# Forward sweeps traced half a step earlier, two products ahead of the retention scores, and a bfloat16 column sum in the up projection

## The chip, the cores and the metric

One core of a Trainium2 chip runs the kernel. The metric is the device time of one execution in microseconds (us). The engines are named as in the profile: PE (TensorE matmul) and PEld (its weight loads), DVE (VectorE), ACT (ScalarE), POOL (GpSimd), SP (SyncE, which issues most transfers).

## What is computed

One block of a diffusion transformer, 2048 tokens of width 1024, with 256 context tokens. The mixer has four HGRN2 heads and four retention heads of width 128, and each head runs in both directions over the sequence. In outline:

```python
hx = rmsnorm(x, norm1_g) * (1 + sc1) + sh1            # modulated by c
feats = split(hx @ w_in)                              # q, v, gates of 4 HGRN2 and 4 retention heads
states = context_states(features of ctx)              # start states of both directions
o_f = chunk_scan(q, k, v, decay, s_f)                 # forward over the chunks
o_b = flip(chunk_scan(flip(q), flip(k), ...))         # backward
hg = rmsnorm((o_f + o_b) * sigmoid(gate)); ret = rmsnorm(y_f + y_b) * silu(gate)
x = x + g1 * (concat(hg, ret) @ w_out)
h2 = rmsnorm(x, norm2_g) * (1 + sc2) + sh2
x = x + g2 * ((silu(conv3(h2 @ w_gate)) * (h2 @ w_up)) @ w_down)
return rmsnorm(x, final_g)
```

## The kernel before

**Arithmetic.** A large product is made of pairs of float16 parts, three matmuls to a product (lines 88 to 90), and a 2x2 blocked product is done with seven block products (`unit`, `head_unit`, `ffn_unit`: products 0 to 6). Each weight is scaled by a power of two that is found from the sum of its squares: ACT squares it and accumulates a column of sums (one for each half of the weight), PE adds the column over the partitions (`allsum`, line 111, one float32 matmul with a matrix of ones for each column), and five short DVE operations make the power of two (`pow2`, lines 99 to 103).

**The heads.** A head's sequence is cut into four groups of 512 tokens. `heads` runs 32 steps, s = 4h + i: head h (0 to 3 HGRN2, 4 to 7 retention), step i of it. Step (h, i) is called h.i here. A step has three strands:

- the backward sweep of head h over group 3 - i (`hg_sweep1`, `ret_sweep1`; a generator that yields about 14 times for HGRN2 and 8 times for retention). The retention one begins with the scores (`rsc`, line 1207), the HGRN2 one with seven levels of products with K and Q (lines 837, 844, 848, 853). It leaves the output so far in a tile `ou`, the query in `qf`.
- the forward sweep of the head before, h - 1, over group i. Its first half (`hg_sweep2`, `ret_sweep2`) takes the forward state through the group (four DVE operations of line 907, eight instructions of line 905 on PE), adds the result to `ou` (line 932 or 1241), gates it (933, HGRN2), and sends it through four squares on ACT (917) and six POOL operations for the norm (`rstd`, lines 71 to 76). Its second half (`hg_sweep2b`, `ret_sweep2b`) multiplies by the norm on DVE (line 939, or four of line 1248), transposes on PE (`otp`, line 924), copies on ACT and issues a transfer on ACT's queue.
- the projection of the next step's features (`hg_proj`, `ret_proj`, or `ret_gate` near the end), the filler: a generator of some 14 or 18 products.

`step` makes the first two strands one generator, `weave` lets it run and calls the filler in between, in the proportion n_fill to n_main. `tick` puts in pieces of the next head's weights.

```python
        if prev is not None:
            (self.hg_sweep2 if hgp else self.ret_sweep2)(pool, (h - 1) % NH, i, prev)
        for j in range(3):
            next(main, None)
            yield
        ...
        if prev is not None:
            (self.hg_sweep2b if hgp else self.ret_sweep2b)(pool, (h - 1) % NH, i, prev)
        yield from main
```

What Python traces first has priority, but the order in each engine's queue is made when the program is built, by a scheduler that lets a later operation whose inputs it holds ready pass an earlier one that it holds not ready. Once built, each queue has a fixed order. Tiles of one tag share a few buffers, which come free with the last use: `tu` (three banks of PSUM, used by both sweeps, transposes and sums), `ou` and `qf` (one for each of four slots), `gate` (five).

After the 32 steps four more (head index 8) do the forward sweep of the last head alone. Then come the output projection, the up projection and the down projection.

**The up projection.** `up_weights` prepares the weights of 11 pairs of column blocks, twice each (gate and up), so it is called 22 times: two squares on ACT (line 1483), 16 matmuls of one bfloat16 column on PE (line 1488, `col`), `allsum` of the two columns of sums, the power of two, and the splitting into seven blocks. It runs as background work between the products of `ffn_unit`.

Of the kernel before, what the change touches and what calls it, by code (L numbers as in the profile page):

```python
# [11 lines left out]
BF16 = mybir.dt.bfloat16  # L12
# [3 lines left out]
ALU = mybir.AluOpType  # L16
PSUM = bass.MemoryType.PSUM

P = 128
# [4 lines left out]
NG = SEQ // G  # L24
CT = 256
NH = 4
# [24 lines left out]
def view(t, off, dims):  # L51
    return bass.AP(t.tensor, t.offset + off, [t.ap[0]] + dims)


class Kern:
# [50 lines left out]
    def allsum(self, cols, tag="tu"):  # L106

        o = self.ps(tag, [P, 1], "allsum")
        n = cols.shape[-1]
        for i in range(n):  # L110
            self.nc.tensor.matmul(o, self.onesq, cols[:, i:i + 1], start=i == 0, stop=i == n - 1, skip_group_check=True)
        return o

    def allmax(self, col, tag="tu"):
# [827 lines left out]
        nc.scalar.copy(m, tp.rearrange("p c t -> p (c t)"))  # L942
        nc.scalar.dma_start(self.mixd[h][:, g * G:(g + 1) * G], m)

    def weave(self, main, filler, n_main, n_fill):

        done = 0
        for j, _ in enumerate(main):
            while filler is not None and done * n_main < (j + 1) * n_fill:
                done += 1  # L950
                if next(filler, self) is self:
                    filler = None
        for _ in filler or ():
            pass

    def step(self, h, i, W, cur, prev, pr):

        pool = self.mp
        g = NG - 1 - i
        slot = i if h % 2 == 0 else NG - 1 - i  # L960
        hg, hgp = h < NH, h - 1 < NH
        if h < 2 * NH:
            main = (self.hg_sweep1 if hg else self.ret_sweep1)(pool, h % NH, g, slot, pr, cur)
        else:
            main = iter(())
        if prev is not None:
            (self.hg_sweep2 if hgp else self.ret_sweep2)(pool, (h - 1) % NH, i, prev)
        for j in range(3):
            next(main, None)
            yield  # L970
            if i == 0 and j == (1 if hg else 0) and h < 2 * NH:
                yield from (self.hg_context if hg else self.ret_context)(pool, h % NH, W, cur)
        if h or i:
            self.tick(self.n_tick)
        if prev is not None:
            (self.hg_sweep2b if hgp else self.ret_sweep2b)(pool, (h - 1) % NH, i, prev)
        yield from main
        if h or i:
            self.tick(self.n_tick)

    def heads(self):

        nc, pool = self.nc, self.mp
        W, items = self.W0, self.items0
        self.mod_first()
        items[5][0]()
        place = [self.gate_tile() for _ in range(4)]
        xc = self.load_rows(None, place)
        self.norm_rows(NG - 1, self.x3)
        for _, comp in items[:4]:  # L990
            comp()
        self.lower_bounds()
        self.mod1 = self.modulation(self.ep, pool, view(self.sv, V_N1, [[0, 2], [1, 8]]), self.modT[:, :, 8:16],
                                    self.modT[:, :, 0:8], 0, 1.3)
        ftags = "Kl", "Kl", "qf0", "qf1", "K0", "Q0"
        for _ in self.first_blocks(NG - 1, self.x3, self.places(ftags, "ftmp"), "pj", 1):
            pass
        for _, comp in items[4:]:
            comp()
        for w, dq in W.values():  # L1000
            nc.vector.tensor_tensor(dq, dq, self.dqx[:, 0:1], ALU.mult)
        prev, items = None, []
        cur = dict(grp={}, sg={})
        pr = {}
        first = self.hg_proj(pool, 0, NG - 1, W, pr, cur, True)
        zq = ("z",) * 7 + ("q",)
        rows = lambda g, tags: self.norm_rows(g, self.load_rows(g, [p() for p in self.places(tags, f"x{g}")]))
        x2 = rows(2, zq)
        for _ in self.with_blocks(first, self.first_blocks(2, x2, self.places(ftags, "ftmp"), "tu")):
            pass  # L1010
        Wn = W
        for s in range(4 * 2 * NH):
            h, i = divmod(s, NG)
            hn, inn = divmod(s + 1, NG)
            if i == 0:
                if h < 2 * NH - 1:
                    Wn, items = self.head_weights(h + 1)
                    n = -(-len(items) // 6)
                    if NH <= h < 2 * NH - 1:
                        mods = [it for c in ((4, 5, 6), (7, 8, 9), (10, 11))[h - NH] for it in self.mod_later(c)]  # L1020

                        pairs = [items[k:k + 2] for k in range(0, len(items), 2)]
                        none = [(None, lambda: None)] * 2
                        items = []
                        while pairs or mods:
                            items += (pairs.pop(0) if pairs else none) + (mods[:2] or none)
                            mods = mods[2:]
                        n = 4
                    self.todo += items
                else:  # L1030
                    items = self.out_weights()
                    self.todo += items[:5]
                    n = 1
                self.n_tick = n
            if i == NG - 1:
                while self.todo or self.loaded:
                    self.tick(4)
                if h == 2 * NH - 1:
                    self.todo += items[5:]
            blocks = None  # L1040
            if s == 0:
                for _ in self.first_blocks(None, self.norm_rows(None, xc), self.places(("A", "A", "Ta", "Kl"), "cftmp", 2), "tu"):
                    pass
                blocks = self.first_blocks(1, rows(1, ("ou1", "ou2", "ou3", "q", "qf2")), self.places(zq, "ftmp"), "pj")
            if s == 1:
                blocks = self.first_blocks(0, rows(0, ("ou2", "ou3", "qf2", "gate", "gate", "q")), self.places(zq, "ftmp"), "pj")
            if s == 4 * 2:
                self.ret_consts()
            prn = {}
            nxt = cur if inn else dict(grp={}, sg={})  # L1050
            if hn < 2 * NH:
                filler = (self.hg_proj if hn < NH else self.ret_proj)(pool, hn % NH, NG - 1 - inn, Wn if inn == 0 else W, prn, nxt, *((True,) if blocks else ()))
                if blocks:
                    filler = self.with_blocks(filler, blocks)
            else:
                filler = chain(self.ret_gate(NH - 1, 0, W, cur), self.ret_gate(NH - 1, 1, W, cur))
            self.weave(self.step(h, i, W, cur, prev, pr), filler, (14 if h < NH else 8) + (0 if i else 19 if h < NH else 10),
                       18 if hn < NH else 14 if hn < 2 * NH - 1 else 11 if hn < 2 * NH else 8)
            pr = prn
            if i == NG - 1:  # L1060
                prev, W, cur = cur, Wn, nxt
        for i in range(NG):
            self.weave(self.step(2 * NH, i, None, None, prev, None), self.ret_gate(NH - 1, i + 2, W, prev) if i < 2 else None, 3, 4)
            if i == 1:
                self.mixed_pairs(0)
# [403 lines left out]
    def up_weights(self, j, ty):  # L1469
# [10 lines left out]
        ssq = kp.tile([P, 2], F32, tag="ssqw2", bufs=2, name="ssqw")  # L1480
# [5 lines left out]
        for i in range(2):  # L1486
            for k in range(KT):
                nc.tensor.matmul(col[:, i:i + 1], sqs[i][:, k * P:(k + 1) * P], self.onesb, start=k == 0 and i == 0,
                                 stop=k == KT - 1 and i == 1, skip_group_check=True)
        s, neg, dq = self.scales(self.allsum(ssq, "sc"), self.dqx[:, 1:2], ("dqz", "dqvg")[ty])  # L1490

        if ty == 0:
            tap = kp.tile([P, 2, 3], F32, tag="taps", bufs=2, name="taps")
# [353 lines left out]
```

## Time and profile before

| | |
|---|---|
| median of 3 runs | 2703.32 us (2699.55 to 2703.40) |
| the profiled execution | 2701.94 us, its span 2699.5 us |
| PE busy | 94% of the span |
| heads with a forward sweep, steps 1.0 to 7.3 | 296.9 to 1238.9 us |
| last forward sweep, output projection | 1238.9 to 1521 us |
| up projection (its steady part) | 1521 to 2235 us |
| down projection | 2235 to 2699.5 us |

The boundaries are the first score matmul of a step for the heads, and rounded starts of a stage for the others. Starts and waits below are in us from the span's start. A wait is idle time of an engine just before an instruction, with the instruction that ended it behind the arrow.

### The profile page before, as it was taken

What the parts mean: (1) busy time and instruction counts of PE and PEld (TensorE: products, weight loads), DVE (VectorE), ACT (ScalarE), POOL (GpSimd) and SP (SyncE); (2) the same over time, 40 slices, a digit from 0 to 9 for tenths busy, and PEclk for the clock granted to TensorE, in tenths of its full rate; (3) what the DMA queues carried; (4) which work ended last, traced back from release to release, by engine and by line L of the source; (5) the groups of instructions that cost most, each with busy time, mean ns of one, the idle gap of its engine ahead of it and who ended that gap; (6) DMA issues with size and microseconds to landing.
All of it is one profiled execution on the core that took longest, in us unless ns stands there. A gap on an engine that the chain in (4) does not pass through costs nothing.

```text
span 2699.5 us, 56351 instructions
## 1 busy us (share of the span) xinstructions
PE 2544.2 (94%) x22829; PEld 1680.0 (62%) x22829; DVE 1847.7 (68%) x3585; ACT 1344.8 (50%) x2902; POOL 785.0 (29%) x905
## 2 busy tenths in 40 slices
PE   5798999999999999998999999999999999999998
PEld 2578888888889889886454444444444444444443
DVE  4898677776767686666466788888787777323553
ACT  5776456564555444445455566565555555311120
POOL 3733112111223232221344344343443342000102
PEclk7899999999999999998999999999999999999999
DMA  8224234243337575755521232333322325635552
GB/s 297 104 87 158 96 111 146 88 138 119 121 127 257 197 246 178 239 195 180 196 98 47 94 110 101 107 105 110 117 101 103 118 88 197 254 129 187 203 194 95
DMA packets 213621, 393.98 MB, mean 146 GB/s; under 512 B 15599, under 2 KB 97747, under 8 KB 208752
## 3 DMA queue, kind: packets, MB, share of 16 engines
q1 hardware_dynamic: 203808, 373.42, 40.1%
q10 hardware_dynamic: 9248, 16.79, 1.9%
q8 instruction: 178, 2.92, 0.4%
q14 instruction: 83, 0.68, 0.1%
q0 software_dynamic: 304, 0.17, 0.0%
HBM read 298.57 MB, written 91.75 MB: 145 GB/s over the span
## 4 chain that ended last, share of the span: by engine, by line
PE 71%; DVE 15%; ACT 4%; issue 4%; DMA 3%; POOL 2%; SPq 0%; DVEq 0%; ACTq 0%; POOLq 0%
PE pa L88 8%; PE pa L89 8%; PE pa L90 8%; PE pd L89 5%; PE pd L90 5%; PE pd L88 5%; PE pc L88 4%; PE pc L89 4%; PE pc L90 4%; PE pb L88 2%; PE pb L90 2%; PE pb L89 2%; PE opp L89 2%; PE opp L88 2%; PE opp L90 2%
## 5 line engine op out<-in xcount | busy, mean ns | idle before, releaser
L88 PE MATMUL pa<-feat,w 128*128 128x512 f16 x704 | 267.9, 381 | 12.2 <-ACT ta L549 8.1
L89 PE MATMUL pa<-feat,w 128*128 128x512 f16 x704 | 268.1, 381 | 0.0
L90 PE MATMUL pa<-feat,w 128*128 128x512 f16 x704 | 264.9, 381 | 0.0
L89 PE MATMUL pd<-wd,actl 128*128 128x512 f16 x616 | 233.3, 379 | 0.0
L90 PE MATMUL pd<-wd,actl 128*128 128x512 f16 x616 | 233.3, 379 | 0.0
L88 PE MATMUL pd<-wd,actl 128*128 128x512 f16 x616 | 232.7, 379 | 0.0
L89 PEld LDWEIGHTS <-w 128*128 128x128 f16 x1232 | 120.8, 98 | 155.4 <-issue 15.6
L90 PEld LDWEIGHTS <-w 128*128 128x128 f16 x1232 | 121.4, 99 | 145.1 <-issue 1.4
L88 PEld LDWEIGHTS <-w 128*128 128x128 f16 x1232 | 121.7, 99 | 141.6 <-issue 2.4
L89 PEld LDWEIGHTS <-hx 128*128 128x128 f16 x1824 | 183.0, 100 | 8.5 <-issue 6.3
L90 PEld LDWEIGHTS <-hx 128*128 128x128 f16 x1824 | 182.6, 100 | 3.4 <-issue 2.6
L88 PEld LDWEIGHTS <-hx 128*128 128x128 f16 x1824 | 182.9, 100 | 2.2
L1598 DVE SCALAR_TENSOR_TENSOR st<-act,modT,st 128x512 f16<-128x512 f32 x154 | 144.3, 966 | 32.3 <-ACT st L1597 32.3
L1597 ACT ACTIVATE st<-act,modT 128x512 f16<-128x512 f32 x154 | 107.2, 718 | 83.9 <-DVE act L1587 30.2
L88 PE MATMUL pa<-w_vg,hx 128*128 128x128 f16 x800 | 144.7, 222 | 0.2
L89 PE MATMUL pa<-w_vg,hx 128*128 128x128 f16 x800 | 144.5, 222 | 0.0
L90 PE MATMUL pa<-w_vg,hx 128*128 128x128 f16 x800 | 144.4, 222 | 0.0
L88 PE MATMUL pc<-feat,w 128*128 128x512 f16 x352 | 133.5, 379 | 1.3 <-ACT feat L1372 1.2
L88 PE MATMUL pa<-hx,w_z 128*128 128x256 f16 x464 | 127.6, 275 | 7.5 <-DVE rV L591 4.1
L90 PE MATMUL pc<-feat,w 128*128 128x512 f16 x352 | 133.6, 380 | 0.0
L89 PE MATMUL pc<-feat,w 128*128 128x512 f16 x352 | 133.6, 380 | 0.0
L89 PE MATMUL pa<-hx,w_z 128*128 128x256 f16 x464 | 127.3, 274 | 0.0
(551 smaller groups left out, 7557.6 us busy)
## 6 DMA issues: line engine op xcount, KB each, us to landing
hx<-hxd SPq DMA_DIRECT2D x212, 512.0 KB, 4.7
actd<-st SPq DMA_DIRECT2D x154, 256.0 KB, 2.0
actl<-actd SPq DMA_DIRECT2D x28, 1024.0 KB, 5.0
wur<-in_w_up_dram SPq DMA_DIRECT2D x44, 512.0 KB, 3.9
raw<-in_w_in_dram SPq DMA_DIRECT2D x36, 512.0 KB, 4.6
wm<-in_w_mod_dram SPq DMA_DIRECT2D x64, 256.0 KB, 4.1
hxd<-hx SPq DMA_DIRECT2D x28, 512.0 KB, 3.4
wdb<-in_w_down_dram SPq DMA_DIRECT2D x44, 256.0 KB, 3.9
```

What stands on the lines that cost most here:

```text
L88: mm(ps, lhs(0), rhs(0), start=start, stop=False, skip_group_check=True)
L89: mm(ps, lhs(0), rhs(1), start=False, stop=False, skip_group_check=True)
L90: mm(ps, lhs(1), rhs(0), start=False, stop=stop, skip_group_check=True)
L1597: nc.scalar.activation(p[:, 0], v, AF.Copy, scale=s)
L1598: nc.vector.scalar_tensor_tensor(p[:, 1], v, s, p[:, 0], ALU.mult, ALU.subtract)
```

## The change

- `step`: for heads 1 to 7 the forward sweep of group i + 1 of the head before is traced in step i, not in step i + 1: its first half after the third yield of the backward sweep, its second half at the step's end. Group 0 stays in step 0, where groups 0 and 1 are then both swept, and step 3 has no forward sweep. The four last steps (head index 8) stay as they are.
- `weave`: from head 4 on, two products of the filler are traced before the step's first operation (`lead`), and count as done.
- `up_weights`: the two columns of sums are added on DVE into one bfloat16 column (`both`), and one bfloat16 matmul with ones takes the place of the two float32 ones.

```diff
+    def allsum16(self, cols, tag):
+        both = self.wp.tile([P, 1], BF16, tag="both", bufs=2, name="both")
+        self.nc.vector.tensor_tensor(both, cols[:, 0:1], cols[:, 1:2], ALU.add)
+        o = self.ps(tag, [P, 1], "allsum")
+        self.nc.tensor.matmul(o, view(self.onesb, 0, [[0, P]]), both, start=True, stop=True, skip_group_check=True)
+        return o
...
-    def weave(self, main, filler, n_main, n_fill):
+    def weave(self, main, filler, n_main, n_fill, lead=0):
-        done = 0
+        done = lead
+        for _ in range(lead):
+            next(filler)
...
+        last = h == 2 * NH
+        sweep2, sweep2b = (self.hg_sweep2, self.hg_sweep2b) if hgp else (self.ret_sweep2, self.ret_sweep2b)
+        other = lambda sweep, k: sweep(pool, (h - 1) % NH, k, prev)
-        if prev is not None:
-            (self.hg_sweep2 if hgp else self.ret_sweep2)(pool, (h - 1) % NH, i, prev)
+        if prev is not None and (last or i == 0):
+            other(sweep2, i)
...
-        if prev is not None:
-            (self.hg_sweep2b if hgp else self.ret_sweep2b)(pool, (h - 1) % NH, i, prev)
+        if prev is not None and (last or i == 0):
+            other(sweep2b, i)
+        ahead = prev is not None and not last and i + 1 < NG
+        if ahead:
+            other(sweep2, i + 1)
         yield from main
         if h or i:
             self.tick(self.n_tick)
+        if ahead:
+            other(sweep2b, i + 1)
...
-                       18 if hn < NH else 14 if hn < 2 * NH - 1 else 11 if hn < 2 * NH else 8)
+                       18 if hn < NH else 14 if hn < 2 * NH - 1 else 11 if hn < 2 * NH else 8, 2 if h >= NH else 0)
...
-        s, neg, dq = self.scales(self.allsum(ssq, "sc"), self.dqx[:, 1:2], ("dqz", "dqvg")[ty])
+        s, neg, dq = self.scales(self.allsum16(ssq, "sc"), self.dqx[:, 1:2], ("dqz", "dqvg")[ty])
```

## Rows read from the trace of the kernel before

**Rows 1.** The page: the span, and the busy time of each engine.

```profile
span 2699.5 us, 56351 instructions
PE 2544.2 (94%) x22829; PEld 1680.0 (62%) x22829; DVE 1847.7 (68%) x3585; ACT 1344.8 (50%) x2902; POOL 785.0 (29%) x905
```

**Rows 2.** Windows: length, busy (count) of PE, PEld, DVE, ACT, POOL, clock, DMA.

```profile
296.90:792.00 495.10, 466.08 (x7665) 419.41 (x7665) 347.73 (x795) 274.94 (x688) 89.91 (x108) 0.98 0.37 121
792.00:1238.90 446.90, 422.67 (x5072) 402.23 (x5071) 309.69 (x621) 209.00 (x522) 120.22 (x131) 0.98 0.64 213
1521.00:2235.00 714.00, 709.93 (x3599) 330.57 (x3598) 574.99 (x995) 413.86 (x722) 288.92 (x192) 1.00 0.32 108
```

**Rows 3.** Waits of PE, HGRN and retention stretch: total us, times, longest.

```profile
PE sc L837 <- DVE Q L853: 10.2, 3, 3.4
PE otp L924 <- DVE ou L939: 3.2, 3, 1.9
...
PE otp L924 <- DVE ou L1248: 2.3, 1, 2.3
PE otp L924 <- DVE p2t L99: 1.6, 1, 1.6
PE rsc L1207 <- ACT rV L589: 0.7, 1, 0.7
```

**Rows 4.** Line 111 from 1400 us on: ns min/median/max, first, last start.

```profile
L111 PE MATMUL allsum<-ssqw,ones x88: 250/250/373, 1403.7 to 2228.9; 128*128 128x1 f32 x88
```

**Rows 5.** Timeline of PE at one up-projection call: start us, us, what, count.

```profile
1657.56 0.47 PE L1488 MATMUL col<-onesb,w 128*128 128x1 bf16 x13
1657.89 0.58 PE L111 MATMUL allsum<-ssqw,ones 128*128 128x1 f32 x4
1658.34 0.38 PE L90 MATMUL pb<-feat,w 128*128 128x512 f16 x1
```

**Rows 6.** Timeline of ACT and DVE at that call and the one before.

```profile
1632.08 2.06 DVE L1598 SCALAR_TENSOR_TENSOR st<-act,modT,st 128x512 f16<-128x512 f32 x3
...
1656.25 0.19 ACT L1483 ACTIVATION_READ_ACCUMULATOR w<-wur 128x1 f32 x1
1657.65 0.75 DVE L1567 SCALAR_TENSOR_TENSOR act<-ta,taps,act 128x511 f32<-128x511 f32 x1 [1.94 <-ACT act L1562]
```

**Rows 7.** Lines 907, 932, 1241 on DVE: ns min/median/max, first, last start.

```profile
L907 DVE SCALAR_TENSOR_TENSOR ou<-ou,T x32: 338/346/352, 301.7 to 825.2; 128x128 f32<-128x128 f32 x32
...
L932 DVE TENSOR_TENSOR ou<-ou,o x16: 672/679/689, 307.6 to 895.9; 128x512 f32<-128x512 f32 x16
...
L1241 DVE SCALAR_TENSOR_TENSOR ou<-o,qd,ou x16: 736/742/752, 912.1 to 1275.5; 128x512 f32<-128x512 f32 x16
```

**Rows 8.** Waits of DVE, 792 to 1238.9: total us, times, longest.

```profile
DVE ou L1248 <- POOL rs_y L76: 12.9, 10, 2.6
```

**Rows 9.** Windows by step: 2.0, 3.0, 3.1, 3.3 (HGRN), 5.0, 5.1 (retention).

```profile
463.30:519.30 56.00, 51.08 (x801) 46.21 (x800) 37.68 (x110) 36.43 (x96) 3.81 (x7) 1.00 0.23 73
626.50:680.20 53.70, 53.70 (x816) 48.60 (x815) 31.79 (x90) 23.17 (x62) 3.29 (x7) 1.00 0.23 78
680.20:719.10 38.90, 35.37 (x585) 32.02 (x584) 30.61 (x64) 20.59 (x52) 11.71 (x11) 0.96 0.39 130
...
755.00:792.00 37.00, 34.42 (x610) 31.20 (x609) 23.00 (x43) 18.57 (x47) 4.35 (x7) 1.00 0.41 141
...
908.90:941.10 32.20, 32.20 (x415) 31.13 (x414) 16.46 (x37) 12.69 (x34) 5.32 (x7) 1.00 0.46 150
941.10:971.80 30.70, 27.97 (x334) 26.11 (x333) 27.91 (x49) 14.77 (x35) 11.77 (x11) 1.00 0.73 252
```

**Rows 10.** Timeline of PE at the start of retention step 5.1.

```profile
938.59 0.27 PE L88 MATMUL pa<-hx,w_z 128*128 128x256 f16 x1
...
940.99 0.27 PE L89 MATMUL pb<-hx,w_z 128*128 128x256 f16 x1
941.10 1.06 PE L1207 MATMUL rsc<-K 128*128 128x128 f32 x8
```

More of the change, by code (lines that the diff above doesn't have):

```diff
@@ L961, in step @@
         hg, hgp = h < NH, h - 1 < NH
-        if h < 2 * NH:
+        last = h == 2 * NH
+        sweep2, sweep2b = (self.hg_sweep2, self.hg_sweep2b) if hgp else (self.ret_sweep2, self.ret_sweep2b)
+        other = lambda sweep, k: sweep(pool, (h - 1) % NH, k, prev)
+        if not last:
             main = (self.hg_sweep1 if hg else self.ret_sweep1)(pool, h % NH, g, slot, pr, cur)
@@ L970, in step @@
             yield
-            if i == 0 and j == (1 if hg else 0) and h < 2 * NH:
+            if i == 0 and j == (1 if hg else 0) and not last:
                 yield from (self.hg_context if hg else self.ret_context)(pool, h % NH, W, cur)
```

## The prediction, made before the result was known

> **What bounds the kernel now.** I read the page first, then the stages by windows, then PE's waits by stage, and only then single stretches of the timeline. PE is busy 94% of the span, the next engine, DVE, 68% [rows 1]. A change can therefore shorten the kernel in two ways: by taking PE work away, or by removing time in which PE stands still. The windows show how much there is of the second [rows 2]. In the up projection PE is busy 709.93 of 714.00 us at granted clock 1.00, so a stage with no gaps to close; only less work helps there. In the heads with forward sweeps it is busy 466.08 of 495.10 us (HGRN2) and 422.67 of 446.90 us (retention): 29.0 + 24.2 = 53.2 us idle. That is the whole stock from which moving the sweeps can take. The waits say which of it hangs on a forward sweep [rows 3]: the transpose `otp` of the second half waited for DVE for 3.2 us in the HGRN2 stretch and for 2.3 + 1.6 us in the retention one, 7.1 us together. The larger row of the HGRN2 stretch, 10.2 us for the level products behind line 853, is not the sweep's own wait; it is DVE being late with the levels.
>
> **The column sum, step by step.** The page has 88 float32 matmuls of `allsum` in this part, so four for each of the 22 calls [rows 4]: two columns, two instructions each. What they cost is read from starts, not from their 250 ns, because matmuls overlap. At one call the group of four starts at 1657.89 and the next product's matmul at 1658.34: 0.45 us of PE's queue [rows 5]. Just before, 13 `col` matmuls (bfloat16, one column, 128x128 weights, the same shape as the new one) take from 1657.56 to 1657.89, 0.33 us, 0.025 us each. The new sum is one such matmul. It saves 0.45 - 0.025 = 0.42 us a call, 22 x 0.42 = 9.2 us, and since PE has no gaps there, all of it is span. [...]
>
> The new DVE operation, one column wide, is of the size of the small ones of the power of two. DVE is busy 574.99 of 714.00 us in this stage [rows 2], so its own time is covered by 139 us of DVE idle. What counts is that the sum now waits for DVE, where before it waited for ACT alone. In half of the calls (gate side) the second square's sum is read at 1656.25 + 0.19 = 1656.44, PE comes to the sum at 1657.89, and DVE stands idle for 1.94 us up to 1657.65 [rows 6]: the addition fits in, if it stands there in DVE's queue. In the other half DVE is in a run of 0.7 us operations (three in 2.06 us) when PE arrives [rows 6]; the addition's inputs are ready long before, so it can stand earlier, but the queue's order decides. Bounds for this wait: nothing, or one such operation for 11 calls, 11 x 0.7 = 7.7 us; nothing excludes more. I take 1 us in all, near the lower end, since the sum was traced behind 16 `col` matmuls which PE reaches late.
>
> **The sweeps.** Nothing is added: the same operations stand elsewhere. A sweep costs DVE four state operations of 0.346 us and an addition of 0.679 or 0.742 us [rows 7], and then either two more 512-wide ones (HGRN2, about 0.68 each by line 932) or four more of 128 columns (retention, about 0.346 each): 3.4 to 3.5 us. For heads 1 to 7, step 0 gets a second sweep and step 3 loses its own; steps 1 and 2 keep one. Step 0 can take it: in 3.0 PE is busy all of 53.70 us with DVE at 31.79 (59%), in 5.0 all of 32.20 us with DVE at 16.46 (51%); 2.0, where PE has 4.9 us idle, is the exception [rows 9]. Step 3 is where PE idles (3.3: 37.00 - 34.42 = 2.6 us) with DVE far from full. So the two-sweep step is covered by PE's own products.
>
> The second gain is the distance between halves. DVE waits for POOL's norm before the second half: 12.9 us over ten waits in the retention stretch [rows 8], and everything behind it in DVE's queue waits too. The halves were three yields apart and are now the rest of a step apart (five yields of eight for retention, eleven of fourteen for HGRN2), so the norm should mostly be there. With it go the `otp` waits of 7.1 us. A slot's `ou` and `qf`, and the gates, also come free half a step earlier; I price that at nothing, since no row shows PE waiting for them. What is late next? PE's other just-in-time operands, above all the levels behind line 853. I let half come back: -3.6 us. Bounds: nothing, and all 7.1 us plus half of the 10.2 us (the steps that lose first-half sweep work), 12 us. The transfers of the second half are the same four per head on ACT's queue, earlier; PE waits for none of them until the output projection.
>
> **The two products ahead.** Traced earlier does not mean queued earlier. At step 5.1 the first filler product already starts at 938.59, the second runs to 940.99 and the scores start at 941.10 [rows 10]; the scheduler has done it. There is little left to gain: the wait of the scores for the value tile, 0.7 us, is the row for it [rows 3]. With the count started at two, the later calls of the filler fall on the same yields. The filler's loads, seven on SP and two on ACT's queue, move with its first call, by as little. I take nothing; bounds -0.7 and, if the scores come 24 matmuls later than now, 24 x 0.11 = 2.6 us (the spacing in rows 10, 938.59 to 941.10 for 23) in each of 15 steps, of which PE loses nothing as long as it has those matmuls to do.
>
> **The sum.** 2701.94 (the profiled execution) - 9.2 + 1.0 - 3.6 = 2690.1 us. The median of the runs stands 1.4 us above that execution, so against it the forecast is 2691.5; I say 2691.
>
> **Rivals.**
> *Only the sum counts.* The scheduler had put the sweeps where they could go, as it did with the scores, and order changes alone. Then 2701.94 - 9.2 + 1.0 = 2693.7. It lies within the forecast's own range, so I count it there.
> *The sum waits for DVE.* PE takes its matmuls in order: it idled before `otp` with products standing behind it. If `both` comes late by 0.84 us in the 11 up-side calls (a little more than one of the 0.7 us operations), 9.2 us are gone; with no gain from the sweeps the time is about 2702. [...] For it: DVE at 81% in that stage. Against: inputs ready early.
> *The sweep pushes the levels back.* The first half now stands before level 4 of HGRN2, or before the backward states of retention, in steps where DVE is nearly full: 79% in 3.1, 91% in 5.1 [rows 9]. If its 3.4 us delay what PE waits for, the 14 steps 1 and 2 of heads 1 to 7 pay. From 9.2 / 14 = 0.66 us a step the kernel is no faster; from (9.2 + 5.4) / 14 = 1.04 us it is slower than can be missed; at half the sweep's work, 1.7 us, the time is 2701.94 - 9.2 + 24 = 2717. Against it: these steps carried one sweep before too, at their beginning, and lose that one.
> *The heads give more.* The `otp` waits go whole and DVE, freed from the norm's waits, is in time for half of the level waits: 2701.94 - 9.2 - 12.2 = 2680.5.
>
> **How the numbers follow.** A difference of 0.2%, 5.4 us, is about what a measurement of this kernel can tell from no change. Forecast (2684 to 2698): 0.52. More from the heads (2676 to 2684): 0.18. Gain cancelled (2698 to 2708), by the sum's wait or by small losses in the levels: 0.18. Slower: 0.12. The range 2679 to 2703 leaves out the slower case and the outer parts of its neighbours, about 0.2. Faster is the forecast and the larger gain with a little taken off for a queue order that is new everywhere behind the first change: 0.69; same 0.19; slower 0.12.
>
> **What would show it.** In the profile after: 22 matmuls of the new line, each some 0.03 us apart from its neighbours, and no PE wait on `both`; the up projection shorter by 8 to 9 us; no `otp` waits on line 939 or 1248 in steps 1 to 3 of heads 1 to 7; DVE's waits for the norm smaller by half; PE idle in the heads at 45 to 50 us, against 53.2. The prediction is wrong if PE idles before the new sum for more than 0.4 us a call, if the level waits grow by more than the `otp` waits shrink, or if a half-clock stretch comes in or goes with the new order.

## The result and the profile after

The changed kernel took 2706.90 us (median of 20 runs, 2698.91 to 2713.83) beside 2701.53 us of the kernel before on the same chip (20 runs): ratio 1.0022, 95% interval 1.0013 to 1.0032. The forecast was 2691 us, 0.4% faster; it is 0.2% slower. The profiled execution, 2701.38 us, lies 5.5 us below that median, so its stretches show the losses rather too small.

The page of the changed kernel, span and PE's busy time (before: [rows 1]):

```profile
span 2699.6 us, 56237 instructions
...
PE 2535.8 (94%) x22763; PEld 1670.8 (62%) x22763; DVE 1851.3 (69%) x3607; ACT 1341.1 (50%) x2902; POOL 789.5 (29%) x905
```

Windows of the same three stretches (HGRN2 heads, retention heads, up projection; columns as in [rows 2]):

```profile
297.30:789.80 492.50, 464.30 (x7665) 417.00 (x7665) 343.17 (x795) 273.92 (x688) 90.40 (x108) 0.99 0.37 122
789.80:1244.40 454.60, 425.12 (x5058) 404.48 (x5057) 308.03 (x610) 208.18 (x520) 119.58 (x131) 0.97 0.63 209
1529.50:2235.10 705.60, 700.42 (x3521) 321.27 (x3520) 579.71 (x1014) 411.35 (x722) 291.15 (x192) 1.00 0.32 109
```

Against [rows 2] the HGRN2 heads gave 2.6 us and the up projection 8.4 us, close to what was forecast. The retention heads lost 7.7 us, and the lone last sweep behind them went from 22.9 (1238.9 to 1261.8) to 26.3 us (1244.4 to 1270.7). That is the whole account: 11.0 us gained, 11.1 us lost in this execution.

The clock column belongs to that account. In the retention heads nearly the same matmuls kept PE busy 2.4 us longer (425.12 for 422.67) at a granted clock of 0.97 for 0.98; the other 5.3 of the 7.7 us are idle time (29.5 for 24.2). In the HGRN2 heads PE was busy 1.8 us less, at 0.99 for 0.98, and its idle time hardly moved (28.2 for 29.0): most of that gain is shorter busy time and not closed gaps. In both traces the granted clock stands at 1.00 or at 0.50. Added up from them, 0.50 held for 17 us of the HGRN2 heads before and 7 us after, and for 14 us of the retention heads before and 24 us after. The four stretches at 0.50 in the HGRN2 heads before lie at waits of PE of 2.8 to 3.4 us, the two after at waits of 2.0 and 2.8 us. One place in the HGRN2 heads, before and after (PE's timeline, then a window; the clock is the third number from the end):

```profile
541.15 0.65 PE L837 MATMUL sc<-Q,Kl 128*32 128x32 f32 x32 [3.27 <-DVE Q L853]
541.00:544.30 3.30, 3.15 (x57) 3.09 (x58) 3.30 (x8) 0.85 (x1) 0.55 (x3) 0.50 0.24 70
```
```profile
539.53 0.46 PE L845 MATMUL sc<-Q,Kl 128*32 128x32 f32 x32 [1.98 <-DVE Q L861]
536.00:545.00 9.00, 6.54 (x135) 6.14 (x133) 9.00 (x12) 4.85 (x15) 7.63 (x8) 1.00 0.65 208
```

The waits of PE in the HGRN2 stretch (first line) and the retention stretch (the other two), against [rows 3]:

```profile
PE sc L845 <- DVE Q L861: 9.0, 7, 2.0
...
PE rob L1246 <- DVE Kt L1248: 12.2, 8, 3.0
PE pa L88 <- DVE rV L599: 11.0, 3, 4.8
```

The last two before, which [rows 3] doesn't show:

```profile
PE pa L88 <- DVE rV L591: 4.1, 2, 2.1
PE rob L1227 <- DVE Kt L1229: 3.0, 5, 1.2
```

The level waits `sc` of the HGRN2 heads add up to nearly what they did (9.0 for 10.2 us), but the longest is 2.0 us in place of 3.4. No `otp` wait is left in the retention stretch, as forecast. In their place PE waits 12.2 us for the small updates `Kt` of the backward state (3.0 before) and 11.0 us for the eviction of the value tile `rV` (4.1 before). Both are DVE's work; so the question is what DVE waited for:

```profile
DVE Q L1194 <- DMA sin<-in_rope_dram: 16.4, 6, 3.6
...
DVE ou L1267 <- POOL rs_y L76: 12.5, 10, 2.7
```

The second line is [rows 8] unchanged (12.9), where half was forecast. The first line is new: before, DVE never waited for the sine table. One case from end to end, in the timelines of ACT (two lines; ACTq is its issue of a transfer), DVE, POOL and PE:

```profile
986.15 0.59 ACT L1270 COPY m<-otp 128x512 f32<-128x512 f32 x1 [0.41 <-PE otp L932]
986.21 0.33 ACTq L1182 DMA_DIRECT2D sin<-in_rope_dram  x1
...
991.19 1.22 DVE L1194 TENSOR_TENSOR Q<-K,sin 64x1024 f32<-64x1024 f32 x1 [3.04 <-DMA sin<-in_rope_dram]
...
992.52 2.13 DVE L671 TENSOR_TENSOR dq<-p2i,dqx 128x1 f32<-128x1 f32 x1
...
995.95 0.34 DVE L1248 SCALAR_TENSOR_TENSOR Kt<-rSb,cd,rup 128x128 f32<-128x128 f32 x1
...
991.33 3.30 POOL L1193 TENSOR_TENSOR Q<-K,sin 64x1024 f32<-64x1024 f32 x1 [22.90 <-DMA sin<-in_rope_dram]
...
996.34 0.80 PE L1246 MATMUL rob<-Kt,K 128*128 128x128 f32 x2 [3.01 <-DVE Kt L1248]
```

Read it downwards. The sweep's transposed output is copied to its store tile `m`; the next step's sine table is issued only then, and 4.98 us later DVE may multiply. DVE stood still for 3.04 us, its later work stood behind, and PE waited 3.01 us for `Kt`. A window shows what came with that wait:

```profile
995.40:1002.10 6.70, 5.76 (x39) 5.70 (x40) 6.30 (x14) 2.51 (x10) 0.68 (x1) 0.50 0.43 139
```

Of the five stretches at 0.50 in the retention heads three lie at waits of `rob` for `Kt` (1.92, 3.01 and 2.28 us) and two at waits for `rV` (4.80 and 4.79 us). So more was lost here than idle time: 5.3 us more of it went with a stretch that is 7.7 us longer.

In the kernel before, the table that was issued at 957.16 was used at 979.52, 22 us later, and DVE was waiting for something else:

```profile
957.16 0.33 ACTq L1163 DMA_DIRECT2D sin<-in_rope_dram  x1
...
979.52 1.22 DVE L1175 TENSOR_TENSOR Q<-K,sin 64x1024 f32<-64x1024 f32 x1 [2.29 <-ACT K L589]
```

`sin` and `m` share one tag, `Kl`, with three buffers, handed out in the order of tracing. Before, a step's table was traced between the two halves of the sweep, ahead of the store. In the changed kernel the store at the end of a step is traced first, and the table, which the filler asks for at the start of the next step, comes behind it. The six loads that DVE waited for were issued 3.9 to 6.8 us ahead of their use and took about 4.8 us to land (the median of all 16); before, all 16 were issued 13 to 29 us ahead.

The column sum did what was said of it (lines and durations, then PE's timeline at one call; compare [rows 4] and [rows 5]):

```profile
L117 DVE TENSOR_TENSOR both<-ssqw x22: 147/184/1227, 1392.7 to 2205.1; 128x1 bf16<-128x1 f32 x22
L119 PE MATMUL allsum<-both,onesb x22: 163/163/165, 1412.6 to 2228.9; 128*128 128x1 bf16 x22
```
```profile
1665.44 0.49 PE L1507 MATMUL col<-onesb,w 128*128 128x1 bf16 x14
1665.80 0.16 PE L119 MATMUL allsum<-both,onesb 128*128 128x1 bf16 x1
1665.82 0.38 PE L88 MATMUL pb<-feat,w 128*128 128x512 f16 x1
```

From the sum to the next product it is 0.02 us, and no wait of PE for `both` is in the list of waits. The 14 `col` matmuls start within 0.36 us, 0.026 us apart, which agrees with the 0.025 us of the prediction.

### The profile page after: what moved, and what is told of

Same layout as the page of the kernel before. It is cut to its first block, busy times and chain, and to the rows that moved or that the text cites. A ratio compares the mean times of both kernels' runs of the same rounds, so it can differ in the third digit from the quotient of the medians.

```text
span 2699.6 us, 56237 instructions
## 1 busy us (share of the span) xinstructions
PE 2535.8 (94%) x22763; PEld 1670.8 (62%) x22763; DVE 1851.3 (69%) x3607; ACT 1341.1 (50%) x2902; POOL 789.5 (29%) x905
## 4 chain that ended last, share of the span: by engine, by line
PE 68%; DVE 16%; DMA 5%; issue 4%; ACT 4%; POOL 3%; SPq 0%; DVEq 0%; POOLq 0%; ACTq 0%
PE pa L88 8%; PE pa L89 7%; PE pa L90 7%; PE pd L90 5%; PE pd L89 5%; PE pd L88 5%; PE pc L88 3%; PE pc L90 3%; PE pc L89 3%; PE pb L88 2%; PE pb L89 2%; PE pb L90 2%; PE opp L88 2%; PE opp L89 2%; PE opp L90 2%
## 5 line engine op out<-in xcount | busy, mean ns | idle before, releaser
L88 PE MATMUL pa<-feat,w 128*128 128x512 f16 x704 | 264.5, 381 | 12.1 <-ACT ta L557 8.5
L1617 DVE SCALAR_TENSOR_TENSOR st<-act,modT,st 128x512 f16<-128x512 f32 x154 | 143.3, 967 | 24.9 <-ACT st L1616 24.2
L88 PE MATMUL pa<-hx,w_z 128*128 128x256 f16 x464 | 127.9, 276 | 16.6 <-DVE rV L599 11.0
L89 PEld LDWEIGHTS <-w_z 128*128 128x128 f16 x1072 | 108.0, 101 | 45.0 <-issue 33.8
```

The source lines that it names most:

```text
L88: mm(ps, lhs(0), rhs(0), start=start, stop=False, skip_group_check=True)
L89: mm(ps, lhs(0), rhs(1), start=False, stop=False, skip_group_check=True)
L1617: nc.vector.scalar_tensor_tensor(p[:, 1], v, s, p[:, 0], ALU.mult, ALU.subtract)
```

## The experiments

There were eighteen runs, of sixteen kernels; none leaves out any of the work. The table names them by the first part of their names (e1 is e1_sum_only). Ratios are to the kernel before on the same chip; the last four columns are single profiled executions, in us: the retention heads, how long the clock was at 0.50 in them, the lone last sweep, and the up projection from its first product to the down projection.

| run | what it is | ratio, interval | ret. | at 0.50 | last | up |
|---|---|---|---|---|---|---|
| (before) | | 1 | 446.9 | 14 | 22.9 | 840.3 |
| (changed) | sum, sweeps, lead | 1.0022, 1.0013 to 1.0032 | 454.6 | 24 | 26.3 | 831.9 |
| e1 | sum alone | 0.9987, 0.9977 to 0.9997 | 444.1 | 7 | 23.3 | 838.4 |
| e9 | e1 again | 0.9980, 0.9971 to 0.9988 | 444.7 | 10 | 22.7 | 835.6 |
| e2 | sweeps alone | 1.0047, 1.0035 to 1.0059 | 456.5 | 24 | 27.0 | 840.4 |
| e3 | lead of two alone | 1.0054, 1.0039 to 1.0069 | 458.2 | 20 | 23.1 | 841.4 |
| e18 | lead of one alone | 0.9996, 0.9987 to 1.0006 | 445.9 | 13 | 22.9 | 841.2 |
| e4 | changed, `m` in `qf` | 1.0000, 0.9991 to 1.0009 | 450.7 | 14 | 23.6 | 836.8 |
| e7 | e4 without the lead | 1.0008, 0.9998 to 1.0018 | 457.3 | 24 | 23.7 | 836.9 |
| e5 | sum, `m` in `qf` | 0.9969, 0.9957 to 0.9981 | 445.6 | 10 | 22.4 | 830.3 |
| e6 | sum, sweeps in HGRN2 heads | 0.9964, 0.9952 to 0.9976 | 446.5 | 14 | 22.8 | 834.0 |
| e10 | e6 again | 0.9966, 0.9957 to 0.9976 | 443.6 | 10 | 22.8 | 834.5 |
| e8 | e6, `m` in `qf` | 0.9980, 0.9970 to 0.9989 | 453.8 | 24 | 23.0 | 835.4 |
| e11 | e5, first halves early | 1.0000, 0.9989 to 1.0010 | 443.5 | 10 | 24.9 | 833.7 |
| e12 | e5, second halves early | 1.0043, 1.0030 to 1.0055 | 467.2 | 30 | 24.1 | 830.1 |
| e13 | changed, sine first | 0.9968, 0.9956 to 0.9980 | 444.0 | 14 | 25.8 | 830.1 |
| e14 | e13 without the lead | 0.9971, 0.9960 to 0.9983 | 447.5 | 17 | 29.8 | 831.1 |
| e15 | e3, sine product on POOL | 1.0029, 1.0019 to 1.0039 | 455.1 | 14 | 24.4 | 838.7 |
| e16 | changed, sine product on POOL | 1.0021, 1.0011 to 1.0031 | 454.4 | 17 | 24.6 | 834.9 |
| e17 | sweeps alone, sine first | 1.0012, 1.0003 to 1.0021 | 443.6 | 14 | 27.9 | 840.9 |

(The profiled execution of e11 lies 8.4 us below its median, that of e13 6.3, that of e16 5.7 and that of the changed kernel 5.5: their stages look better than they mostly are.) In the expectations theory A is the late sine table; what a rival's letter stands for is worded beside it.

**The parts one by one.** e1 is the kernel before with the call of `allsum16`:

```diff
-        s, neg, dq = self.scales(self.allsum(ssq, "sc"), ...)
+        s, neg, dq = self.scales(self.allsum16(ssq, "sc"), ...)
```

> The kernel before with the bfloat16 column sum alone. All theories: the up projection is shorter by 8 to 9 us and no wait of PE on the DVE addition appears, so about 2701.5 - 8.5 = 2693 us. If the sum itself were the loss (PE held behind the addition), the time would stay at 2701 or above.

e2 has the edit of `step` alone, e3 that of `weave` alone:

```diff
+        ahead = prev is not None and not last and i + 1 < NG
+        if ahead:
+            other(sweep2, i + 1)
...
+        if ahead:
+            other(sweep2b, i + 1)
```

> The kernel before with the earlier forward sweeps alone. Theory A (the load of the rope's sine table gets behind the sweep's transpose on ACT's queue, because the sweep's output tile and the table share three buffers that are handed out in the order of tracing): the retention stretch (first scores of 4.0 to first operation of the last sweep) is 5 to 10 us longer than the 447 us of before, DVE waits 10 to 20 us for the table, and the time is 2706 to 2716. Theory B (DVE's sweep work delays what PE waits for, the load has nothing to do with it): the same time, but DVE's waits for the table stay small. Theory C (the two products ahead are the loss): at most 2701, DVE's wait for the table near nothing.

```diff
+        for _ in range(lead):
+            next(filler)
```

> The kernel before with the two products ahead alone. Theories A and B: the queues hardly change, 2698 to 2704 us, no DVE wait for the sine table above 3 us. Theory C: 2706 us or more.

The sum alone gained 0.13%, not the 0.30% of the forecast (8.2 us). PE's busy time in its stage fell by 6.9 us (826.3 to 819.4), but PE then stood 5 us longer (19.0 for 14.0) before products whose inputs were not yet there. Waits of PE in e1's up projection:

```profile
PE pa L88 <- ACT ta L557: 10.4, 7, 5.6
PE col L1496 <- ACT w L1491: 3.3, 1, 3.3
```

The `col` wait, for the square that feeds the sum, is not in the changed kernel's up projection, which took 831.9 us against 838.4 here. The same edit is thus worth 2 to 10 us, by the order that the queues got around it and from one execution to the next (profiled stages with the sum: 830.1 to 838.4; without it: 838.7 to 841.4).

Sweeps and lead each lose half a per cent alone, but together, with the sum, 0.22%. So they don't add. e2 has the sine wait (14.3 us over 6); e3 has none. What e3 has is one wait of 5.12 us, seen in the timelines of DVE and PE:

```profile
834.93 2.83 DVE L649 SCALAR_TENSOR_TENSOR w_z<-raw,p2s,w_z 128x512 f16<-128x512 f32 x1
837.80 2.17 DVE L1177 TENSOR_TENSOR Q<-K,sin 64x1024 f32<-64x1024 f32 x1
...
840.67 0.34 DVE L1231 SCALAR_TENSOR_TENSOR Kt<-rSb,cd,rup 128x128 f32<-128x128 f32 x1
...
841.07 0.80 PE L1229 MATMUL rob<-Kt,K 128*128 128x128 f32 x2 [5.12 <-DVE Kt L1231]
```

The update `Kt`, 0.34 us, stands in DVE's queue behind 5 us of weight splitting and of the sine product. From 839.7 to 846.5 the clock was at 0.50. With two products done ahead, fewer stood in PE's queue before the second pair of `rob` to cover the wait; this is the likely reason, but no run shows it.

**The store in another buffer.** e4 gives the store tile the head's own `qf`, whose content is no longer needed:

```diff
-        m = pool.tile([P, G], F32, tag="Kl", bufs=KL, name="m")
+        m = r["qf"]
```

> The changed kernel with one thing more: the sweep's transposed output is stored from the query's tile of its slot, for every head, so that it takes no buffer of the tag that the sine table uses. Theory A: the table is loaded long before its use, DVE's wait for it goes from 16 us to under 3, the retention stretch falls from 455 to 447 us or less, and the time is 2690 to 2698. Theory B: the table's wait goes but the stretch stays within 3 us of 455, and the time at 2702 to 2707.

The sine wait went and with it the loss; but a new wait came. ACT, writing the next head's `qf`, now waits until the store has read it (e4):

```profile
ACT qf L1233 <- DMA mixd<-qf: 31.0, 13, 4.5
```

So e4 (1.0000, 450.7 us) lies in neither theory's range and does not settle theory A by itself. It does settle what held the load: still traced behind the stores, but with no buffer in common with them, the 16 loads were issued 21 to 89 us ahead of their use. e5 has the same edit without sweeps and lead, e7 is e4 without the lead:

> Kernel before with only the one-product sum, and every stored tile m written into the head's own q buffer instead of one of the three shared buffers. Theory A (the sine table's load waits for m's buffer only because the forward sweep was moved): before, the sine table was issued 15 to 24 us ahead of its multiply, so the store's buffer is worth nothing here: ratio as with the sum alone, 0.9975 to 0.9997, retention's heads within 1.5 us of 446.9. Rival (the store's buffer is a gain by itself, whatever the sweeps do): retention's heads 443 or less, ratio 0.9965 to 0.998.

> The changed kernel without the lead, with the stored tile in the head's own q buffer (as in the run e4_store_from_qf, which has the lead). Theory (sweeps and lead each move products against the chain Kt to rob; with the sine table out of the way the lead is the part that still costs): retention's heads 447 to 449 against 450.7 with the lead, ratio 0.9975 to 0.9992. Rival (the early sweep alone is what costs; the lead is neutral beside it): retention's heads 450 to 453, ratio 0.9995 to 1.001. Third: the lead makes good part of what the sweep costs: retention over 453, ratio over 1.001.

e5 is faster than the sum alone (0.9969 against 0.9987 and 0.9980), outside theory A's range and inside the rival's (its retention heads, 445.6 us, are in theory A's), so the buffer is perhaps a gain by itself; as the HGRN2 kernels below lose by it, that is hardly more than what a new order brings. e7's ratio is that of the rival (the lead is neutral beside the early sweep; 0.0008 from e4 is within what the intervals allow), its retention stretch that of the third case. Its profile shows where the wait for the store goes on, from ACT to DVE's `Kt`:

```profile
DVE Kt L1248 <- ACT ou L1236: 15.5, 11, 2.9
```

**The sweeps by head.** e6 moves the sweep only while the current head is HGRN2, without the lead; e8 is e6 with `m` in `qf`; e9 and e10 are e1 and e6 again, side by side:

```diff
-        ahead = prev is not None and not last and i + 1 < NG
+        ahead = prev is not None and h < NH and i + 1 < NG
```

> The changed kernel without the lead, and with the forward sweep half a step sooner only while the head that is being projected and scored is an HGRN head (steps 1.0 to 3.3); retention's steps as in the kernel before; the one-product sum stays. Theory (the changed kernel gains in the HGRN heads, where no sine table is loaded, and loses in the retention heads): HGRN heads 492.5 (2.6 less than before), retention's heads 446 to 448.5, last sweep to out projection 23 us, ratio 0.9965 to 0.9987. Rival (what the HGRN heads gain is handed back at the next stage, since the retention heads' order moves with it): retention 449 or more, ratio 0.9985 to 1.000.

> The run e6_hgrn_sweeps_only, with the stored tile in the head's own q buffer as well. If the store's buffer only undoes what early sweeps do to the sine table, this run equals e6 within 0.0005. If it is a gain by itself, it is faster by 0.001 or more.

> The kernel of the run e1_sum_only a second time, beside the next one. In the up projection its engines have the same order of instructions as those of e6_hgrn_sweeps_only, and yet the profiled stage took 838.36 there and 834.05 here. If that difference belongs to the execution and not to the kernel, this run's ratio is near the middle of the two, 0.997 to 0.9985, its stage anywhere from 833 to 839. If it belongs to the kernel, the ratio is 0.998 to 0.9995 again.

> The kernel of the run e6_hgrn_sweeps_only a second time. If the early sweep in the HGRN heads is worth something (2.6 us in the changed kernel's profile), it is ahead of e9_sum_only_again by 0.0010 or more; if it is worth nothing (495.2 against 495.1 in its own profile), the two are within 0.0008 of each other.

e9's ratio, 0.9980, lies in both ranges and so decides nothing; but the same kernel's stage took 838.4 us in e1 and 835.6 in e9, so 2.8 of the 4.4 us between e1 and e6 can belong to the execution alone. e10 is ahead of e9 by 0.0014 (3.8 us between the medians): the early sweep is worth that much where no sine table is loaded. Not by closing gaps: in the HGRN2 heads PE idles 29.6 us in e10 and 27.6 in e9, and is busy 463.5 and 467.4 us, with 7 and 20 us at 0.50. Windows of e10, HGRN2 and retention heads, each shorter than in [rows 2]:

```profile
298.60:791.70 493.10, 463.50 (x7666) 417.05 (x7666) 342.97 (x795) 274.53 (x688) 90.28 (x108) 0.99 0.38 122
791.70:1235.20 443.50, 420.82 (x5070) 400.64 (x5070) 309.34 (x620) 208.84 (x522) 120.03 (x131) 0.99 0.65 215
```

e6, the same kernel, had 495.2 us in the HGRN2 heads, as before, and e8 came out slower than e6 by 0.0016, with 453.8 us in retention, where it should have changed nothing but a buffer. Against e5, which is traced the same way there, 1.9 of the 8.2 us more are idle time and 6.3 are PE's busy time (428.2 for 421.8), with 24 us at 0.50 in place of 10. Why the clock fell so often in e8, with hardly more idle time, stays open.

**The halves.** e11 moves the first half of the sweep alone, e12 brings the second half right behind the first, both in retention's steps of e5:

```diff
 e11:  if ahead: other(sweep2, i + 1)            # sweep2b(i) stays where it was
 e12:  other(sweep2, i); if soon: other(sweep2b, i)
```

> The run e5_sum_and_store (0.9969, retention's heads 447.6), with only the first half of the sweep moved, in retention's steps alone: the state's four products, four updates and the add are traced half a step sooner, the second half (gate, transpose, store) stays. Theory (the sweep's updates and its add come ahead of the eviction of rV and of the update Kt on VectorE, whose products wait for those): most of what the early sweep costs is here, retention 451 to 457, waits of pa for rV of over 4 us as in e7_no_lead, ratio 0.9985 to 1.001. Rival (the transposes and the gate are what holds): retention 446 to 449, ratio 0.9960 to 0.9978.

> The run e5_sum_and_store, with only the second half of the sweep moved, in retention's steps alone: the gate's four products, the transposes and the store are traced right behind the first half instead of a few products later. Theory (the first half is what costs): retention 446 to 450, ratio 0.9960 to 0.9982. Rival (the second half costs, by the wait for the root on GpSimd that stands ahead of the gate): more than 2 us of new waits on VectorE for rs_y, retention over 451, ratio over 0.9985.

Both cost, 0.31 and 0.74% against e5, so that neither half alone is the cause. (The 447.6 us given for e5 are a misreading, it is 445.6.) The waits for the norm that e12's rival named did not grow (14.5 us, 18.6 in e5). It is again the chain of `Kt` that PE waits for:

```profile
PE rob L1244 <- DVE Kt L1246: 11.5, 5, 4.0
```

Both have the store in `qf`, whose wait on ACT is 21.1 us in e12, so they are no clean measure of the sweep.

**The sine table first.** e13 is the changed kernel with one thing moved: the table for the next projection is loaded just ahead of the early store, into the same three buffers. e14 takes the lead out of e13, e17 the sum as well:

```diff
         if ahead:
+            if NH <= h and hn < 2 * NH:      # hn, inn: the step whose features come next
+                self.sine = pool.tile([P, G], F32, tag="Kl", bufs=KL, name="sin")
+                self.nc.scalar.dma_start(self.sine, rope[:, 1, group of inn])
             other(sweep2b, i + 1)
```

> The changed kernel, with the sine table's load traced just ahead of the early sweep's store, so that it takes its buffer and its place on ScalarE's queue before it; the store keeps its own buffer, and nothing else is edited. Theory A (the sine table, late by the moved sweep, is the largest new loss): VectorE's waits for it go from 16.4 us to under 4, retention's heads from 454.6 to 447 to 451, ratio 0.9985 to 1.0005. Rival B (the sine wait only stood where VectorE would have waited for something else): the wait goes, retention stays at 453 to 457, ratio 1.0012 to 1.003.

> The run e13_sine_first without the lead. If the lead is harmless beside the early sweeps (the run e4_store_from_qf against e7_no_lead: 1.0000 against 1.0008), this is within 0.001 of e13. If the lead costs here what it costs alone (1.0054), this is faster than e13 by 0.003 or more.

> The early sweeps alone (no lead, the column sum as before), with the sine table's load traced ahead of the early sweep's store. By itself the moved sweep cost 0.47% (e2_sweeps_only). If the sine table is all of that cost and the sweep's own gain is the 3.6 us of the forecast, the ratio is 0.998 to 0.9995, retention's heads 444 to 449. If the early sweep costs by something else as well, it is 1.000 to 1.003.

e13 decides. 1.0022 becomes 0.9968, better than expected: 0.54%, or 14.6 us, each against the kernel before on its own chip (the medians, 2694.82 and 2706.90 us, are 12.1 us apart). e17 against e2 is the same edit a second time, 1.0047 to 1.0012. The retention window of e13, its waits of DVE (the sine is in none of the lines; the largest is 15.5 us for the key) and of PE:

```profile
790.10:1234.10 444.00, 418.96 (x5049) 398.48 (x5048) 303.42 (x615) 209.00 (x519) 122.26 (x131) 0.98 0.64 214
```
```profile
DVE Q L1200 <- ACT K L597: 15.5, 10, 2.0
...
PE pa L88 <- DVE rV L599: 10.9, 3, 4.8
...
PE rob L1252 <- DVE Kt L1254: 3.2, 3, 2.2
```

`rob` waits 3.2 us in place of 12.2: that was the sine's part. Against the changed kernel the stretch is 10.6 us shorter: 4.4 us of it are PE's idle time (25.0 for 29.5) and 6.2 its busy time (418.96 for 425.12), with 14 us at 0.50 in place of 24. The two stretches at 0.50 behind the waits for `rV` are still there, the three at `rob` are gone, and one elsewhere is new. The `rV` waits, 10.9, are untouched: they belong to the early sweep, and the kernel is 0.3% faster than before in spite of them. Without the lead nothing changes (0.9971): beside early sweeps it is harmless and useless.

e17 gives the early sweeps' own worth: 1.0012. Against e2 the retention heads went from 456.5 to 443.6 us, 3.3 us below those of the kernel before, and the HGRN2 heads are 2.0 us shorter. But the lone last sweep hands it back, 27.9 for 22.9 us. Its window and PE's wait there:

```profile
1234.10:1262.00 27.90, 17.33 (x232) 16.39 (x230) 19.91 (x74) 16.39 (x43) 3.99 (x12) 0.87 0.42 137
```
```profile
PE otp L932 <- DVE ou L1273: 9.2, 2, 7.5
```

The heads ended 4.8 us earlier than before, and yet the second-last transposes began at 1258.9 against 1258.8. e10, which leaves retention's sweeps where they were, has 22.8 us there. Why the sweep of the last head, whose place in the trace is not edited, ends no sooner stays open; it was not tried. Nor do the parts add here: e14, which is e17 with the sum, is at 0.9971, 0.41% below e17, where the sum alone gave 0.13 and 0.20%.

**The queue, and the lead by dose.** e15 and e16 give DVE's half of the sine product to POOL, in e3 and in the changed kernel; e18 is e3 with one product in place of two:

```diff
-        nc.vector.tensor_tensor(pt[:64], qk[64:], sines[64:], ALU.mult)
+        nc.gpsimd.tensor_tensor(pt[:64], qk[64:], sines[64:], ALU.mult)
```

> The run e3_lead_only (1.0054), with VectorE's half of the sine product given to GpSimd, which then does both halves. Theory (the lead leaves fewer products between the pairs of rob, and the small updates Kt stand in VectorE's queue behind the sine product of 2.17 us and the splits of the weights): the wait of rob for Kt at 841 falls from 5.1 to 3.0 or less, the waits for Kt in retention from 8.1 to under 5, ratio 1.000 to 1.004. Rival (what is late there is ScalarE or the splits alone): the wait stays at 5, ratio 1.0045 or more; GpSimd's longer product may make it worse.

> The changed kernel with both halves of the sine product on GpSimd: the wait for the sine table then no longer stands in VectorE's queue, though the table is as late as before. Theory A (the late table costs because VectorE's updates and evictions queue behind the waiting product): the waits of pa for rV fall from 11.0 to under 7, ratio 0.999 to 1.001. Rival B (the late table itself holds the scores of the next step): ratio 1.002 or more, with waits of rsc for K.

> The lead alone, of one product in place of two. If each product that is traced ahead takes cover from the products rob at the step's end, half of the cost stays: ratio 1.0015 to 1.004 (two: 1.0054), waits of rob for Kt between 3.0 (before) and 8.1 (two). If the cost of two is one of a particular order of VectorE's queue, this run may come out anywhere from 0.999 to 1.006, with other waits at its head.

e15 missed: the product of 2.17 us left DVE's queue, and the two splits that remained took 5.58 us while POOL did its two halves (2.41 and 2.69 us), so the wait at the same place was 4.2 us and not under 3; the ratio, 1.0029, is in the theory's range all the same, about half of e3's loss. In e16 the waits of `rob` for `Kt` fell to 4.7 us, but those for `rV` rose to 13.4 and the time stayed: POOL does both halves one behind the other, and later work waited for it, the scores `rsc` for `K` too (3.6 us, 3 times). That is what rival B foretold, so the loss does not hang on DVE's queue alone. The late table was not mended by letting another engine wait for it (1.0021 beside 1.0022). e18 shows no dose: one product ahead costs nothing (0.9996), two cost 0.54%. Nor is the sum of the waits for `Kt` the cause, 7.2 us in e18 and 8.1 in e3; the longest is 2.6 us in e18 and 5.1 in e3. The lead's loss probably belongs to the particular order of the queues that came of it; this was not shown.

## Why the prediction was wrong

**The column sum: right in the changed kernel, about half of it alone.** Term -9.2 + 1.0 = -8.2 us; the window gave -8.4 in the changed kernel, with PE's busy time down by 9.5 (709.93 to 700.42) and no wait for `both`. Alone it gave 0.13 and 0.20%, some 3.5 and 5.4 us: its gain depends on its surroundings by more than the 1 us allowed for waits.

**The sweeps' own gain: right in sign, not in place, and not by the mechanism.** Term -3.6 us, by closed gaps. In the HGRN2 heads it was -2.6 in the changed kernel, and e10 against e9 says 3.8; but PE's idle time there stayed at 28 to 30 us, and what fell was its busy time, with the longest level waits (3.4 to 2.0 us) and the time at 0.50. The size was luck. The `otp` waits left the retention steps. But DVE's wait for the norm did not shrink (12.5 for 12.9), PE's idle time in the heads went to 57.7 us (28.2 + 29.5) in place of 45 to 50, and in retention the gain was handed back in the last sweep (e17).

**The step that failed** is the one priced at nothing in two sentences: that the filler's loads "move with its first call, by as little", and that of the second half's transfers "PE waits for none". Neither looked at what the store and a load of the filler have in common: the three buffers of `Kl`, which e4 shows to be what held the load back, and ACT's queue. The store was moved past the load, the load came some 5 us ahead of its use where it had 22, and it takes about as long. With the load put first and nothing else of the change touched, 12.1 of the 15.9 us between forecast and measurement came back (e13): 2694.8 us, inside the forecast's range. The prediction's own last sign of being wrong came true as well: stretches at half clock came in with the new order in retention (14 to 24 us) and went in the HGRN2 heads (17 to 7). Its sums counted a wait at its length and had no term for them; in e13 against the changed kernel PE's busy time is 6.2 of the 10.6 us.

**The two products ahead: right beside the sweeps, by luck.** Nothing was taken, and nothing it is in e13 against e14 and in e4 against e7. By itself, which the forecast didn't ask, it costs 0.54%: the bound of 2.6 us a step was for scores that come later, and what came later in the one long wait was `Kt`. Why two products cost this and one nothing stays open.

**The rivals.** The slower one priced DVE's work of the sweep in front of the levels. Not that work but a late load, which DVE's queue stood behind, was it, in retention alone. The rival of a late `both` did not come.

## What to carry to other kernels

When a step moves, list every tile it takes from a shared tag and every load that takes from the same tag: the order in which they are traced is part of the change, and a load that slips behind a store loses its head start without anyone having moved it (here from 22 us to some 5). Read for each load the time from its issue to its first use, before pricing the move at nothing. Read the granted clock of a stretch beside PE's idle time: here, with nearly the same matmuls, its busy time changed along with it (425.12 us at 0.97 in the changed kernel's retention heads, 418.96 at 0.98 in e13's). An edit that only reorders is worth trying part by part and stage by stage: here the sum with the early sweeps in the HGRN2 heads alone (0.9964 and 0.9966), or the whole change with the load put first (0.9968), beat both kernels, and the difference between those two is not measurable.

## What the runs showed of the hardware

More than its own length can be lost at a short wait of PE. In the changed kernel's retention heads all five stretches at a granted clock of 0.50 lie at waits of 1.9 to 4.8 us. Behind the wait of 3.01 us the float16 products of 128 columns started 0.107 us apart (25 from 999.07 to 1001.63, at 0.50); the next ones of that shape started 0.056 us apart (24 from 1002.55 to 1003.84, at 1.00). But not every such wait has a stretch at 0.50 behind it (the level wait of 1.98 us above has none), and idle time alone doesn't tell how much of that there will be (e8: 25.7 us idle, 24 at 0.50; e15: 32.1 idle, 14 at 0.50).

A one-column operation can take as long as a large one. In the changed kernel `dq`, 128x1, took 2.13 us at 992.52, until 994.65, and POOL's product of 3.30 us from 991.33 ended at 994.63; all 40 in the kernel before took 0.15 us (ns min/median/max):

```profile
L663 DVE TENSOR_TENSOR dq<-p2i,dqx x40: 145/149/151, 227.3 to 2231.8; 128x1 f32<-128x1 f32 x40
```

The same came once more, at 867.72: 2.13 us, until 869.85, beside POOL's product of 3.30 us from 866.53. Both times POOL had begun 1.19 us earlier, and `dq` ended 0.02 us behind it; the median of the 40 is 0.15 us here too. What held `dq` was not shown.

The same kernel doesn't take the same time twice. e1 and e9 are one kernel, and their up projection took 838.4 and 835.6 us; e6 and e10 are another, and their HGRN2 heads took 495.2 and 493.1 us. Profiled executions lay up to 8.4 us from their kernel's median. A stage's difference of 2 or 3 us between two single profiles decides nothing here by itself.
